# Two tiles of heads in one burst of the scan's products, in a one-core decoder trunk

## The chip, the core and the metric

The kernel runs on one core of a Trainium2 chip. The metric is the time of one execution on the device in microseconds (us), the median of several runs. TensorE does the matmuls (PE in the rows; PEld is its weight load), VectorE (DVE), ScalarE (ACT) and GpSimd (POOL) the elementwise work, and the queue of SyncE (SP) issues the DMAs.

## What is computed

Two layers over 512 tokens of width 2048. The first has a Mamba-2 mixer, the second stick-breaking attention; after each mixer comes a gated embedding. The change is in the first layer's mixer, which has 8 groups of 8 heads of 64 channels and works in 4 chunks of 128 tokens. Cut to what matters of the reference:

```
scores = einsum("bclgn,bcsgn->bclsg", cm, bm)
y_diag = einsum("bclsg,bclsgr,bcsgrp->bclgrp", scores, decay, xdt)
chunk_states = einsum("bclgn,bclgr,bclgrp->bcgrpn", bm, decay_to_end, xdt)
prev_states = scan(state * chunk_decay + chunk_states)
y_off = einsum("bclgn,bcgrpn,bclgr->bclgrp", cm, prev_states, exp(acum))
y = (y_diag + y_off + d_skip * xs) * silu(z)
y = y * rsqrt(mean(y * y over the group) + eps) * gnorm_w;  out = y @ out_w
```

`decay` is exp of the difference of two cumulative sums where the row is not before the column, else 0.

## The kernel before

All activations lie with channels on the partitions and the 512 tokens along the free dimension. A projection is split into units: one unit makes 128 output channels, and has 16 blocks of 128 input channels, each with three matmuls of 512 columns (high and low parts of weight and activation in fp32r, `mm3`). Weights come in halves of 8 blocks (512 KB, `block`): a DMA into `raw` (two buffers), a cast by ScalarE to `wh`, a difference by VectorE to `wl` (three buffers each). These matmuls write tiles named mm.

The order on TensorE is written out by hand by the class `Flow`. It queues every matmul behind the one before, counts a planned time for each (512/2370 = 0.216 for an mm or for a product in fp32 of 128 columns; one product in fp32 shows as two MATMULs in the trace), and after every three mm asks its jobs (`poll`). A job is a generator: it yields a planned delay and is resumed at the first poll after it. The delay counts from before the resumed piece of work. The order of the other engines' instructions, and of the DMAs on SP's queue, is set by the framework's scheduler.

For each group of heads the loop does units for B, C and four tiles of x (`conv`), then spawns the job `scan`, and goes on with four units for the gate z (`zs[0]` to `zs[3]`), the next group's units or, after the last group, the first half of the output projection `w_out`, whose activations `staged` loads back from DRAM (y_d), into the buffers of xc. So the scan's pieces of work lie between mm of other units.

The scan transposes x (px_x), makes the scores (px_sc), transposes B (px_bt) and makes the states (px_st, kept as `sts`). Then, for each of four tiles `i` of two heads each:

- for each of two heads: a DMA of one row of `ac_d`, broadcast to all partitions, into `ab` (two buffers); M by ScalarE from it (L411 four times, L414), times the masked scores scT by VectorE (L415); half of `eA` by ScalarE (L417, two buffers). M has four buffers, which the group norm's `sh` and `sl` share.
- a delay of 9.0, and a wait until `zs[i]` is there;
- a burst on TensorE: 8 products of y (px_y, 64 weight columns each, two heads side by side) and 3 of the states (px_o);
- eA times px_o (VectorE, L433), `y` from xc and px_y (VectorE, L436), their sum (GpSimd, L437), times zs (VectorE, L438), its square (ScalarE) and the sum of squares `sacc` (GpSimd).

After the four tiles come a delay of 8.5, one of 3.5, and the group norm (px_gn). All px tiles share four PSUM buffers of one bank each.

Of the kernel before, what the change touches and what calls it, by code (L numbers as in the profile page):

```python
# [9 lines left out]
F32 = mybir.dt.float32  # L10
F32R = mybir.dt.float32r
AF = mybir.ActivationFunctionType
ALU = mybir.AluOpType
# [3 lines left out]
P = 128  # L17
T = 512
# [3 lines left out]
HG = 8  # L22
NH = 64
NC = 4
# [58 lines left out]
def trunk(  # L83
    ctx: ExitStack, tc: tile.TileContext, xT, pT, vecs, hvecs, consts, w_dt, w_in, w_out, w_sb, w_v, w_sbo, w_gate, w_ple, out
):
    nc = tc.nc
    V, S, G = nc.vector, nc.scalar, nc.gpsimd
    fl = Flow(tc)
# [11 lines left out]
    ac_d = dram.tile([NH, T], F32, name="ac_d")  # L100
    h_d = dram.tile([EARLY * P, T], F32, name="h_d")

    def px(name="px"):
        return pxp.tile([P, T], F32, tag="px", name=name)
# [14 lines left out]
    dsk = vec[:, 96:128]  # L119
# [20 lines left out]
    def split(dst_h, dst_l, src, scale=None):  # L140
        if scale is None:
            S.copy(dst_h, src)  # L142
            V.tensor_tensor(dst_l, src, dst_h.bitcast(F32), op=ALU.subtract)  # L143
        else:
            S.activation(dst_h, src, AF.Copy, scale=scale)
            V.scalar_tensor_tensor(dst_l, src, scale, dst_h.bitcast(F32), op0=ALU.mult, op1=ALU.subtract)  # L146
# [73 lines left out]
    with ExitStack() as st:  # L220
        sp = st.enter_context(tc.tile_pool(name="sp", bufs=1))

        def tmp(name):
            return sp.tile([P, T], F32, tag="tmp", name=name, bufs=3)
# [4 lines left out]
        for k in range(KT):  # L229
# [16 lines left out]
            else:  # L246
                sq = tmp("sq")
# [22 lines left out]
        act_ = sp.tile([P, NC, NH], F32, name="act_")  # L270
# [71 lines left out]
        def scan(g, BT, CT, xc, zs):  # L342

            hs = slice(g * HG, (g + 1) * HG)
            yield 11.0
            xdt, xw = [], []
            for c in range(NC):
                pt = px("px_x")
                for i in range(4):
                    fl.transpose(pt[:, i * P : (i + 1) * P], xc[i][:, c * P : (c + 1) * P], ident)  # L350
                xd = sp.tile([P, HG, 64], F32, tag=f"xdt{c}", name=f"xdt{c}")
                V.tensor_tensor(
                    xd,
                    pt.rearrange("p (h q) -> p h q", q=64),
                    dtt[:, c, hs].unsqueeze(2).broadcast_to([P, HG, 64]),
                    op=ALU.mult,
                )
                xdt.append(xd)
                if c < NC - 1:
                    w_ = sp.tile([P, HG, 64], F32, tag="xw", name="xw")  # L360
                    G.tensor_tensor(w_, xd, dte[:, c, hs].unsqueeze(2).broadcast_to([P, HG, 64]), op=ALU.mult)
                    wh_ = sp.tile([P, T], F32R, tag="xwh", name="xwh")
                    wl_ = sp.tile([P, T], F32R, tag="xwl", name="xwl")
                    split(wh_, wl_, w_.rearrange("p h q -> p (h q)"))
                    xw.append((wh_, wl_))
                if c == 1:

                    pss = px("px_sc")
                    for c_ in range(NC):
                        cs = slice(c_ * P, (c_ + 1) * P)  # L370
                        fl.mm(pss[:, cs], BT[:, cs], CT[:, cs])
                    scT = sp.tile([P, NC, P], F32, tag="scT", name="scT")
                    V.tensor_tensor(
                        scT, pss.rearrange("p (c l) -> p c l", l=P), tri.unsqueeze(1).broadcast_to([P, NC, P]), op=ALU.mult
                    )
                    psb = px("px_bt")
                    for c_ in range(NC - 1):
                        fl.transpose(psb[:, c_ * P : (c_ + 1) * P], BT[:, c_ * P : (c_ + 1) * P], ident)
                    Bh = sp.tile([P, (NC - 1) * P], F32R, tag="Bh", name="Bh")
                    Bl = sp.tile([P, (NC - 1) * P], F32R, tag="Bl", name="Bl")  # L380
                    split(Bh, Bl, psb[:, : (NC - 1) * P])
                yield 4.0
                if c >= 1:

                    e = c - 1
                    pst = px("px_st")
                    es = slice(e * P, (e + 1) * P)
                    mm3(pst, Bh[:, es], Bl[:, es], xw[e][0], xw[e][1])
                    sc = sp.tile([P, HG, 64], F32, tag=f"st{e}", name=f"st{e}")
                    if e == 0:  # L390
                        sts = [sc]
                        V.tensor_copy(sc, pst.rearrange("p (h q) -> p h q", q=64))
                    else:
                        G.tensor_tensor(sc, sts[-1], cdb[:, e, hs].unsqueeze(2).broadcast_to([P, HG, 64]), op=ALU.mult)
                        V.tensor_tensor(sc, pst.rearrange("p (h q) -> p h q", q=64), sc, op=ALU.add)
                        sts.append(sc)
                    yield 1.0

            sacc = sp.tile([P, T], F32, tag="sacc", name="sacc")
            ys = []  # L400
            for i in range(4):
                eA = sp.tile([P, T - P], F32, tag="eA", name="eA", bufs=2)
                Ms = []
                for hh in range(2):
                    h = g * HG + 2 * i + hh
                    ab = sp.tile([P, T], F32, tag="ab", name="ab", bufs=2)
                    nc.sync.dma_start(ab, ac_d[h : h + 1, :].broadcast_to([P, T]))
                    M = sp.tile([P, NC, P], F32, tag="Mt", name="M", bufs=4)

                    for c in range(NC):  # L410
                        S.activation(  # L411
                            M[:, c, :], ab[:, c * P : (c + 1) * P], AF.Relu, bias=act_[:, c, h : h + 1], scale=-1.0
                        )
                    S.activation(M, M, AF.Exp, scale=-1.0)  # L414
                    V.tensor_tensor(M, M, scT, op=ALU.mult)  # L415
                    pp = slice(64 * hh, 64 * hh + 64)
                    S.activation(eA[pp, :], ab[pp, P:], AF.Exp)  # L417
                    Ms.append(M)
                yield 9.0
                while zs[i] is None:  # L420
                    yield 1.0
                psy = px("px_y")
                for c in range(NC):
                    for hh in range(2):
                        fl.mm(psy[64 * hh : 64 * hh + 64, c * P : (c + 1) * P], xdt[c][:, 2 * i + hh, :], Ms[hh][:, c, :])
                pso = px("px_o")
                for c in range(1, NC):
                    fl.mm(
                        pso[:, (c - 1) * P : c * P],
                        sts[c - 1].rearrange("p h q -> p (h q)")[:, i * P : (i + 1) * P],  # L430
                        CT[:, c * P : (c + 1) * P],
                    )
                V.tensor_tensor(eA, pso[:, : T - P], eA, op=ALU.mult)  # L433
                y = sp.tile([P, T], F32, tag="y", name="y", bufs=2)
                u = 4 * g + i
                V.scalar_tensor_tensor(y, xc[i], dsk[:, u : u + 1], psy, op0=ALU.mult, op1=ALU.add)  # L436
                G.tensor_tensor(y[:, P:], y[:, P:], eA, op=ALU.add)  # L437
                V.tensor_tensor(zs[i], y, zs[i], op=ALU.mult)  # L438
                ys.append(zs[i])
                if i == 0:  # L440
                    S.activation(sacc, ys[i], AF.Square)
                else:
                    sq = tmp("sq")
                    S.activation(sq, ys[i], AF.Square)
                    G.tensor_tensor(sacc, sacc, sq, op=ALU.add)
            yield 8.5
            psn = px("px_gn")
            sh = sp.tile([P, T], F32R, tag="Mt", name="sh", bufs=4)
            sl = sp.tile([P, T], F32R, tag="Mt", name="sl", bufs=4)
            split(sh, sl, sacc)  # L450
            yield 3.5
            mm2(psn, r512, sh, sl)
            rg = sp.tile([P, T], F32, tag="rg", name="rg")
            rsqrt(rg, psn, eps6[:, 1:2])
            for i in range(4):
                u = 4 * g + i
                V.scalar_tensor_tensor(ys[i], ys[i], gnw[:, u : u + 1], rg, op0=ALU.mult, op1=ALU.mult)
                nc.sync.dma_start(y_d[u * P : (u + 1) * P, :], ys[i])

        for g in range(NG):  # L460
            u0, c0 = 10 * g, 6 * g
            BT = sp.tile([P, T], F32, tag="BT", name="BT", bufs=2)
            CT = sp.tile([P, T], F32, tag="CT", name="CT", bufs=2)
# [4 lines left out]
            xc = []  # L468
# [5 lines left out]
            zs = [None] * 4  # L474
# [20 lines left out]
    h = []  # L495
# [316 lines left out]
```

## Time and profile before

| | us |
|---|---|
| median of 3 runs | 2749.87 |
| lowest and highest | 2748.03, 2751.34 |
| profiled execution | 2750.45 |
| its span, first to last instruction | 2748.6 |
| TensorE busy in it | 2729.6 (99%) |
| VectorE, ScalarE, GpSimd busy | 1519.1, 1262.0, 362.1 |

A row of the timeline has start, duration, engine, line, operation, output and inputs, the number of equal instructions in a row, and in brackets the engine's idle time before it with what ended it. Matmuls overlap: the distance of two starts is what TensorE pays, not the duration. Grouped rows have busy time, mean ns of one, and idle time before them.

### The profile page before, as it was taken

The page shows a single profiled execution, that of the slowest core. Times are in us where ns is not written, and L with a number is a line of the kernel's source. Part 1 is how long each engine was busy: PE and PEld are TensorE (multiplying, and loading weights), DVE is VectorE, ACT ScalarE, POOL GpSimd, SP SyncE. Part 2 cuts the span into 40 slices and gives each one's busy share as a digit, 9 for nine tenths or more (in the row PEclk, how much of TensorE's full clock was granted, in tenths as well). Part 3 has the DMA queues.
Part 4 walks back from the last instruction along what each step waited for, and adds up shares of the span by engine and source line. Part 5 has one row for each costly group of instructions (what it writes and reads, how often), then busy time and mean ns, then how long its engine had stood idle before and what let it go on. Part 6 is the DMA issues. An engine that isn't in the chain of part 4 may idle for free.

```text
span 2748.6 us, 32580 instructions
## 1 busy us (share of the span) xinstructions
PE 2729.6 (99%) x12684; PEld 2248.5 (82%) x12684; DVE 1519.1 (55%) x1970; ACT 1262.0 (46%) x1956; POOL 362.1 (13%) x363
## 2 busy tenths in 40 slices
PE   8999999999999999999999999999999999999999
PEld 6888888888888878888888888888888888888887
DVE  8565665665565673342433547647647657643533
ACT  6464545546464552232433436646546546533321
POOL 2222221212222120001100100000000000011000
PEclk9999999999999999999999999999999999999999
DMA  4342333333242446343233322322232322332332
GB/s 160 109 131 93 130 100 123 100 113 124 96 131 98 142 141 222 94 145 93 92 100 100 94 98 90 95 89 91 82 96 85 92 91 86 113 124 97 107 117 90
DMA packets 98346, 300.52 MB, mean 109 GB/s; under 512 B 10960, under 2 KB 11088, under 8 KB 98192
## 3 DMA queue, kind: packets, MB, share of 16 engines
q1 hardware_dynamic: 98192, 298.44, 33.7%
q8 instruction: 99, 1.62, 0.2%
q14 instruction: 55, 0.45, 0.1%
HBM read 280.18 MB, written 18.22 MB: 109 GB/s over the span
## 4 chain that ended last, share of the span: by engine, by line
PE 96%; DMA 1%; DVE 1%; ACT 1%; issue 0%; POOL 0%; SPq 0%; DVEq 0%
PE mm L54 80%; PE pv L54 6%; PE px_p L54 2%; PE px_r L54 1%; PE px_y L54 1%; PE px_z L54 1%; PE px_av L54 1%; PE px_o L54 1%; DMA stg<-y_d 1%; PE px_st L54 1%; PE px_qn L54 1%; PE px_x L57 1%; PE psB L54 0%; PE psd L54 0%; DVE al L146 0%; DVE al L143 0%
## 5 line engine op out<-in xcount | busy, mean ns | idle before, releaser
L54 PE MATMUL mm<-ah,wh 128*128 128x512 f32 x3312 | 1301.0, 393 | 1.7 <-ACT ah L142 1.7
L54 PE MATMUL mm<-ah,wl 128*128 128x512 f32 x3312 | 1292.2, 390 | 0.0
L54 PE MATMUL mm<-al,wh 128*128 128x512 f32 x3312 | 1290.4, 390 | 0.8 <-DVE al L143 0.8
L135 ACT CAST wh<-raw 128x1024 fp32r<-128x1024 f32 x457 | 479.1, 1049 | 840.8 <-PE mm L54 714.2
L137 DVE TENSOR_TENSOR wl<-raw,wh 128x1024 fp32r<-128x1024 f32 x457 | 568.8, 1245 | 530.2 <-ACT wh L135 529.4
L54 PEld LDWEIGHTS mm<-ah,wl 128*128 128x128 f32 x3312 | 621.9, 188 | 132.0
L54 PEld LDWEIGHTS mm<-al,wh 128*128 128x128 f32 x3312 | 622.5, 188 | 129.4 <-DVE al L143 2.1
L54 PEld LDWEIGHTS mm<-ah,wh 128*128 128x128 f32 x3312 | 622.4, 188 | 128.5 <-ACT ah L142 2.8
L503 POOL TENSOR_TENSOR ssq<-ssq,sq 128x512 f32<-128x512 f32 x45 | 71.6, 1590 | 619.9 <-ACT sq L502 619.9
L339 DVE SCALAR_TENSOR_TENSOR cv<-xr,vec,cv 128x512 f32<-128x512 f32 x144 | 108.7, 755 | 2.9
L650 POOL TENSOR_SCALAR_AFFINE_SELECT lm<-lm 128x128 f32<-128x128 f32 x64 | 28.1, 439 | 615.6 <-DVE lm L649 609.8
L54 PE MATMUL pv<-wh,ah 128*128 128x512 f32 x256 | 101.0, 395 | 0.4 <-DVE gt L532 0.4
L54 PE MATMUL pv<-wl,ah 128*128 128x512 f32 x256 | 99.9, 390 | 0.0
L54 PE MATMUL pv<-wh,al 128*128 128x512 f32 x256 | 99.7, 389 | 0.0
L411 ACT ACTIVATE M<-ab,act__370 128x128 f32<-128x128 f32 x256 | 83.7, 389 | 32.5 <-PE px_y L54 31.2
L203 ACT ACTIVATE sg<-cv 128x512 f32<-128x512 f32 x48 | 30.3, 632 | 122.0 <-DVE cv L339 121.8
L532 DVE TENSOR_TENSOR gt<-mm,rbc 128x512 f32<-128x512 f32 x32 | 22.1, 691 | 103.9 <-PE mm L54 103.9
L205 POOL TENSOR_TENSOR xc<-cv,sg 128x512 f32<-128x512 f32 x32 | 42.7, 1334 | 263.8 <-ACT sg L204 263.8
L647 DVE SCALAR_TENSOR_TENSOR lb<-px_z,e 128x128 f32<-128x128 f32 (+1 forms) x64 | 31.4, 490 | 72.7 <-ACT e L645 72.1
L415 DVE TENSOR_TENSOR M<-M,scT 128x512 f32<-128x512 f32 x64 | 58.5, 923 | 14.0 <-ACT M L414 13.8
L205 POOL TENSOR_TENSOR zs<-zs,sg 128x512 f32<-128x512 f32 x32 | 44.7, 1396 | 139.6 <-ACT sg L204 128.7
L335 DVE TENSOR_TENSOR xr<-mm,rbc 128x512 f32<-128x512 f32 x47 | 32.4, 689 | 52.7 <-PE mm L54 52.7
(219 smaller groups left out, 2546.1 us busy)
## 6 DMA issues: line engine op xcount, KB each, us to landing
raw<-in_w_in SPq DMA_DIRECT2D x160, 512.0 KB, 3.6
raw<-in_w_sb SPq DMA_DIRECT2D x96, 512.0 KB, 3.5
raw<-in_w_out SPq DMA_DIRECT2D x64, 512.0 KB, 3.9
raw<-in_w_gate SPq DMA_DIRECT2D x64, 512.0 KB, 3.5
ab<-ac_d SPq DMA_DIRECT2D x64, 256.0 KB, 3.3
raw<-in_w_v SPq DMA_DIRECT2D x32, 512.0 KB, 3.5
raw<-in_w_sbo SPq DMA_DIRECT2D x32, 512.0 KB, 3.5
y_d<-zs SPq DMA_DIRECT2D x32, 256.0 KB, 3.8
```

What stands on the lines that cost most here:

```text
L54: self._queue(self.tc.nc.tensor.matmul(out, lhsT, rhs, start=start, stop=stop), rows / 2370.0)
L135: S.copy(wh, raw)
L137: V.tensor_tensor(wl, raw, wh.bitcast(F32), op=ALU.subtract)
L203: S.activation(tmp, half, AF.Tanh)
L205: G.tensor_tensor(dst, half, tmp, op=ALU.mult)
L335: V.tensor_tensor(xr[:, 3 : T + 3], ps, rbc, op=ALU.mult)
L339: V.scalar_tensor_tensor(cv, xr[:, tap : tap + T], cw[:, u, tap : tap + 1], cv, op0=ALU.mult, op1=ALU.add)
L411: S.activation(M[:, c, :], ab[:, c * P : (c + 1) * P], AF.Relu, bias=act_[:, c, h : h + 1], scale=-1.0)
L415: V.tensor_tensor(M, M, scT, op=ALU.mult)
L503: G.tensor_tensor(ssq, ssq, sq, op=ALU.add)
L647: V.scalar_tensor_tensor(lb, pz, 0.0, e, op0=ALU.min, op1=ALU.subtract)
L650: G.affine_select(out=lm[:, :P], in_=lm[:, :P], compare_op=ALU.is_gt, fill=0.0, base=0, pattern=[[1, P]], channel_multiplier=-1,)
```

## The change

The loop over four tiles becomes a loop over two pairs. M of all four heads of a pair is made first; the delay is 16.0 before the first pair and 18.0 before the second, and the wait is for the second tile's zs. Then one burst has the 8 products of y of the one tile, those of the other, and the 3 products of the states of the one and of the other, in four PSUM tiles. The elementwise work follows for each of the two tiles, with the same instructions. The numbers of buffers stay.

```diff
-            for i in range(4):
-                eA = sp.tile([P, T - P], F32, tag="eA", name="eA", bufs=2)
-                Ms = []
-                for hh in range(2):
...
-                    Ms.append(M)
-                yield 9.0
-                while zs[i] is None:
-                    yield 1.0
-                psy = px("px_y")
-                for c in range(NC):
-                    for hh in range(2):
-                        fl.mm(psy[64 * hh : 64 * hh + 64, c * P : (c + 1) * P], xdt[c][:, 2 * i + hh, :], Ms[hh][:, c, :])
-                pso = px("px_o")
-                for c in range(1, NC):
-                    fl.mm(
-                        pso[:, (c - 1) * P : c * P],
...
-                V.tensor_tensor(eA, pso[:, : T - P], eA, op=ALU.mult)
...
+            for i0 in (0, 2):
+                eAs, Ms = [], []
+                for i in (i0, i0 + 1):
+                    eA = sp.tile([P, T - P], F32, tag="eA", name="eA", bufs=2)
+                    for hh in range(2):
+                        h = g * HG + 2 * i + hh
+                        ab = sp.tile([P, T], F32, tag="ab", name="ab", bufs=2)
+                        nc.sync.dma_start(ab, ac_d[h : h + 1, :].broadcast_to([P, T]))
+                        M = sp.tile([P, NC, P], F32, tag="Mt", name="M", bufs=4)
...
+                        Ms.append(M)
+                    eAs.append(eA)
+                yield 18.0 if i0 else 16.0
+                while zs[i0 + 1] is None:
+                    yield 1.0
+                psys = [px("px_y") for _ in range(2)]
+                for q in range(2):
+                    for c in range(NC):
+                        for hh in range(2):
+                            fl.mm(
+                                psys[q][64 * hh : 64 * hh + 64, c * P : (c + 1) * P],
+                                xdt[c][:, 2 * (i0 + q) + hh, :],
+                                Ms[2 * q + hh][:, c, :],
+                            )
+                psos = [px("px_o") for _ in range(2)]
+                for q in range(2):
+                    for c in range(1, NC):
+                        fl.mm(
+                            psos[q][:, (c - 1) * P : c * P],
...
+                for q in range(2):
+                    i = i0 + q
+                    eA = eAs[q]
+                    V.tensor_tensor(eA, psos[q][:, : T - P], eA, op=ALU.mult)
...
+                    G.tensor_tensor(y[:, P:], y[:, P:], eA, op=ALU.add)
+                    V.tensor_tensor(zs[i], y, zs[i], op=ALU.mult)
...
```

## Rows read from the trace of the kernel before

**Rows 1.** The page: the chain that ended last, by engine.
```profile
PE 96%; DMA 1%; DVE 1%; ACT 1%; issue 0%; POOL 0%; SPq 0%; DVEq 0%
```

**Rows 2.** Timeline of TensorE around the first burst of the fourth group.
```profile
504.58 0.39 PE L54 MATMUL mm<-ah,wl 128*128 128x512 f32 x1
504.90 1.09 PE L54 MATMUL px_y<-M,xdt 128*64 128x128 f32 x16
505.93 0.94 PE L54 MATMUL px_o<-CT,st 128*128 128x128 f32 x6
...
506.93 0.39 PE L54 MATMUL mm<-al,wh 128*128 128x512 f32 x1
...
509.24 0.39 PE L54 MATMUL mm<-ah,wl 128*128 128x512 f32 x1
```

**Rows 3.** Timeline, 444 to 453: first and last of 40 mm.
```profile
444.03 0.39 PE L54 MATMUL mm<-ah,wl 128*128 128x512 f32 x1
...
452.87 0.39 PE L54 MATMUL mm<-ah,wl 128*128 128x512 f32 x1
```

**Rows 4.** Groups by shape on TensorE, whole span: busy us, mean ns, idle us.
```profile
L54 PE MATMUL px_y<-M,xdt 128*64 128x128 f32 x512 | 35.0, 279 | 0.0
L54 PE MATMUL px_o<-CT,st 128*128 128x128 f32 x192 | 29.9, 292 | 0.0
...
L54 PE MATMUL px_sc<-CT,BT 128*128 128x128 f32 x64 | 8.5, 275 | 0.0
```

**Rows 5.** Timeline of TensorE where the scores pass into the transposes of B.
```profile
479.86 1.06 PE L54 MATMUL px_sc<-CT,BT 128*128 128x128 f32 x8
480.75 0.49 PE L57 MATMUL px_bt<-cst,BT 128*128 128x128 f32 x3
```

**Rows 6.** The page: casts of weights by ScalarE; loads of ab, us to landing.
```profile
L135 ACT CAST wh<-raw 128x1024 fp32r<-128x1024 f32 x457 | 479.1, 1049 | 840.8 <-PE mm L54 714.2
...
ab<-ac_d SPq DMA_DIRECT2D x64, 256.0 KB, 3.3
```

**Rows 7.** Timeline of TensorE in the last group's scan.
```profile
994.97 1.09 PE L54 MATMUL px_y<-M,xdt 128*64 128x128 f32 x16
...
1018.13 0.39 PE L54 MATMUL mm<-ah,wl 128*128 128x512 f32 x1
...
1019.78 0.50 PE L54 MATMUL mm<-al,wh 128*128 128x512 f32 x1 [0.33 <-DVE al L143]
```

**Rows 8.** Busy us (instructions) of PE, PEld, DVE, ACT, POOL in one stretch.
```profile
505.90:524.80 18.90, 18.90 (x113) 15.33 (x111) 11.78 (x14) 14.35 (x31) 5.29 (x4) 1.00 0.45 133
```

**Rows 9.** Timeline of ScalarE there: casts of staged tiles.
```profile
1011.00 2.19 ACT L142 CAST ah<-stg 128x512 fp32r<-128x512 f32 x4 [2.26 <-DMA stg<-y_d]
...
1018.27 1.27 ACT L142 CAST ah<-stg 128x512 fp32r<-128x512 f32 x2 [1.10 <-DMA stg<-y_d]
```

**Rows 10.** Instructions that touch M: ns min/median/max, first and last start.
```profile
L415 DVE TENSOR_TENSOR M<-M,scT x64: 675/693/1789, 114.5 to 1022.0; 128x512 f32<-128x512 f32 x64
```

**Rows 11.** Timeline of the vector engines from the same burst on.
```profile
506.03 1.57 ACT L411 ACTIVATE M<-ab,act__370 128x128 f32<-128x128 f32 x5 [1.72 <-PE px_y L54]
...
506.90 0.56 DVE L433 TENSOR_TENSOR eA<-px_o,eA 128x384 f32<-128x384 f32 x1
...
507.51 0.62 ACT L414 ACTIVATE M<-M 128x512 f32<-128x512 f32 x1
507.54 1.02 POOL L437 TENSOR_TENSOR y<-y,eA 128x384 f32<-128x384 f32 x1 [1.87 <-DVE eA L433]
...
508.59 0.53 ACT L417 ACTIVATE eA<-ab 64x384 f32<-64x384 f32 x1 [0.47 <-POOL y L437]
...
515.44 1.28 ACT L411 ACTIVATE M<-ab,act__370 128x128 f32<-128x128 f32 x4 [2.75 <-PE px_y L54]
...
519.46 1.54 POOL L445 TENSOR_TENSOR sacc<-sacc,sq 128x512 f32<-128x512 f32 x1 [1.47 <-ACT sq L444]
...
519.76 1.78 DVE L415 TENSOR_TENSOR M<-M,scT 128x512 f32<-128x512 f32 x1
```

More of the change, by code (lines that the diff above doesn't have):

```diff
@@ L400, in scan @@
             ys = []
-            for i in range(4):
-                eA = sp.tile([P, T - P], F32, tag="eA", name="eA", bufs=2)
-                Ms = []
-                for hh in range(2):
[L405 to L408, printed above, removed]
-                    for c in range(NC):
-                        S.activation(
-                            M[:, c, :], ab[:, c * P : (c + 1) * P], AF.Relu, bias=act_[:, c, h : h + 1], scale=-1.0
-                        )
[L414 to L417, printed above, removed]
-                    Ms.append(M)
-                yield 9.0
-                while zs[i] is None:
-                    yield 1.0
-                psy = px("px_y")
-                for c in range(NC):
-                    for hh in range(2):
-                        fl.mm(psy[64 * hh : 64 * hh + 64, c * P : (c + 1) * P], xdt[c][:, 2 * i + hh, :], Ms[hh][:, c, :])
-                pso = px("px_o")
-                for c in range(1, NC):
-                    fl.mm(
-                        pso[:, (c - 1) * P : c * P],
-                        sts[c - 1].rearrange("p h q -> p (h q)")[:, i * P : (i + 1) * P],
-                        CT[:, c * P : (c + 1) * P],
-                    )
-                V.tensor_tensor(eA, pso[:, : T - P], eA, op=ALU.mult)
[L434 to L445, printed above, removed]
@@ new lines, in scan @@
+            for i0 in (0, 2):
[8 more added lines that the diff above has]
+                        for c in range(NC):
+                            S.activation(
+                                M[:, c, :], ab[:, c * P : (c + 1) * P], AF.Relu, bias=act_[:, c, h : h + 1], scale=-1.0
+                            )
+                        S.activation(M, M, AF.Exp, scale=-1.0)
+                        V.tensor_tensor(M, M, scT, op=ALU.mult)
+                        pp = slice(64 * hh, 64 * hh + 64)
+                        S.activation(eA[pp, :], ab[pp, P:], AF.Exp)
+                        Ms.append(M)
[5 more added lines that the diff above has]
+                for q in range(2):
+                    for c in range(NC):
+                        for hh in range(2):
[3 more added lines that the diff above has]
+                                Ms[2 * q + hh][:, c, :],
+                            )
+                psos = [px("px_o") for _ in range(2)]
[3 more added lines that the diff above has]
+                            psos[q][:, (c - 1) * P : c * P],
+                            sts[c - 1].rearrange("p h q -> p (h q)")[:, (i0 + q) * P : (i0 + q + 1) * P],
+                            CT[:, c * P : (c + 1) * P],
+                        )
+                for q in range(2):
+                    i = i0 + q
+                    eA = eAs[q]
+                    V.tensor_tensor(eA, psos[q][:, : T - P], eA, op=ALU.mult)
+                    y = sp.tile([P, T], F32, tag="y", name="y", bufs=2)
+                    u = 4 * g + i
+                    V.scalar_tensor_tensor(y, xc[i], dsk[:, u : u + 1], psys[q], op0=ALU.mult, op1=ALU.add)
+                    G.tensor_tensor(y[:, P:], y[:, P:], eA, op=ALU.add)
+                    V.tensor_tensor(zs[i], y, zs[i], op=ALU.mult)
+                    ys.append(zs[i])
+                    if i == 0:
+                        S.activation(sacc, ys[i], AF.Square)
+                    else:
+                        sq = tmp("sq")
+                        S.activation(sq, ys[i], AF.Square)
+                        G.tensor_tensor(sacc, sacc, sq, op=ALU.add)
```

## Prediction

> **What bounds the kernel.** I read the chain that ended last first: 96% of it is TensorE, and the vector engines have 1% each [rows 1]. So time is won only where TensorE issues its work faster, or lost where it waits. The profiled run took 2750.45 us for a span of 2748.6, 0.02% above the median of 2749.87; I make the sum in differences and apply it to the median.
>
> The next view is the timeline of TensorE around one burst of the scan [rows 2]. A projection matmul (mm) starts every 0.2267 us where nothing is in its way (39 starts in 8.84 us, [rows 3]). In a burst a product in fp32 appears as two MATMULs: 8 products of y are 16 MATMULs with 64 weight columns, 3 products of the states are 6 MATMULs with 128. From the last mm start before it (504.58) to the second after it (506.93) are 2.35 us; two mm starts would take 0.453, so the burst costs 1.90 us. There are 32 of them (512 MATMULs of px_y, [rows 4]).
>
> **What a burst costs at its borders.** By the grouped lines [rows 4] the 16 MATMULs of px_y are busy 35.0/32 = 1.094 us per burst, so they start (1.094 - 0.273)/15 = 54.7 ns apart. The pace of 128x128 in fp32 I take from px_sc, which comes 8 in a row: (8.5/8 - 0.275)/7 = 112.5 ns. At these paces a burst would be 16 x 0.0547 + 6 x 0.1125 = 1.55 us. So 1.90 - 1.55 = 0.35 us go at its borders, mm to px_y, px_y to px_o, px_o to mm. Is it the change of tile or the change of shape that costs? Where px_sc passes into px_bt [rows 5], output, PSUM buffer and operands change and the shape stays: eight starts, the one over the border among them, take 0.89 us, 0.111 each. So a new tile of the same shape costs nothing there, and what costs in a burst I take to be the change from 128 weight columns to 64 and back.
>
> After a burst mm is slow for a while: the ten starts from 506.93 to 509.24 take 2.31 us in place of 2.27, 0.04 more [rows 2].
>
> **The change, part by part.** The sixteen merged bursts do the same 704 MATMULs. Each merge puts 22 MATMULs inside a burst that exists, at 1.55 us, in place of 1.90 + 0.04 for one of its own.
>
> Borders: 16 x 0.35 = 5.5 us less. From below the border between the two tiles of heads could cost as much as that between shapes (nothing saved); the nearest row [rows 5] has it at nothing, so I take 5.5.
>
> The slow mm after a burst: between 0 and 16 x 0.04 = 0.7 us less. If it grew with the number of MATMULs in the burst, a merge would save none of it. I take it as a price per burst, 0.7, since it is spent after the burst, on mm that are the same either way.
>
> The trace's pace inside a burst stands against the Trainium skill's "TensorE: Matmul & The Clock Gate", section "Back-to-back issue gap", which gives about 81 ns per matmul for a stream of weight loads and matmuls of 128 columns. By that figure 22 MATMULs more would be an estimated 1.78 us, a merge would save 0.16 us and the kernel 2.6; the trace has 54.7 and 112.5 ns for these shapes, and I go by it.
>
> Vector, ScalarE and GpSimd do the same instructions. The eight loads of ab in a group stay too, on SP's queue; the third and fourth of the second half now wait for the first burst. A load of weights queued behind such a wait comes later, and that is hidden: ScalarE's 457 casts of weights stand 714 us, 1.6 each, waiting for TensorE to give back a buffer [rows 6], and with three buffers a cast block is used some two blocks (24 mm, 5.4 us each) after; only a delay beyond that would reach TensorE. PSUM: a merged burst takes all four px buffers; the last product before it (px_st) lies 17 plan us earlier and the next (px_gn) 8.5 + 3.5 later, so none is waited for. Nothing is costed there.
>
> When the bursts come follows from the plan: an mm counts 512/2370 = 0.216 there, three make a step of 0.648. A 16.0 in place of 9.0 is 25 steps for 14, so the first burst of the group of [rows 2] moves from 504.90 by 11 steps, 33 mm, 7.5 us, to 512.4. A merged burst's 22 products count 22 x 0.216 = 4.75 in the plan; of 18.0 there remain 13.25, 21 steps, 63 mm, 14.3 us. With the burst's own 3.5 us the second comes 17.8 us after the first.
>
> The last group is the only place where TensorE already waits in this part: from 1018.13 two starts take 1.65 us in place of 0.45, for the staged tiles of y_d [rows 7], 1.2 us lost. Its first burst, now at 994.97 [rows 7], moves to about 1002.4, the second to 1020.2, and ScalarE must now do, from 1003.6 on (when px_y gives M's buffers back), the work that took it 14.35 busy us in an earlier group [rows 8] and the last seven casts of staged tiles (4, 1 and 2 in three rows, of which [rows 9] has the first and the last), 0.6 each, 4.1 in all. That ends at 1022.0, with the product with scT (0.69 at the median, [rows 10]) at 1022.7; the second half of the burst needs it at 1021.1. So it is 1.6 us late, of which 1.2 is the wait that is there already: 0.4 us more. The bounds: 1.2 less if the staged tiles come in time, 3.3 more if the last staged load slips behind one of ab (both are 256 KB, and ab takes 3.3 us to land, [rows 6]). I take 0.5.
>
> Sum: -5.5 - 0.7 + 0.5 = -5.7; 2749.9 - 5.7 = 2744.2 us.
>
> **Rival 1, slower: the second burst waits for M.** Four M are made between the bursts in place of two, because there are four buffers and all are held until px_y. The path after the first burst's start, by [rows 2, 6, 10, 11]: px_o starts 1.03 us after px_y, now 1.03 + 0.87 = 1.9; the first tile's px_o 0.94; eA on VectorE 0.56; y on GpSimd 1.02; eA on ScalarE 0.53, which frees an ab buffer; the load, 3.3 us to landing; two M at 5 starts in 1.57 us and an exp of 0.62, some 1.8 each, and an eA between, 4.1; a cast of weights 1.0; the product with scT 0.69. With the gaps between them 14.3 us, against 17.8 + 0.9 (the second tile's px_y is half a burst later): over 4 us to spare. By ScalarE's load it is tighter: from 1.13 us after the burst's start to 18.7 are 17.5 us, for 14.35 us of work and 0.69: 2.5 to spare. Against it: in 505.9 to 524.8 that work took 18.9 us with its idle time [rows 8], which would be 2.1 us too late; but 2.75 of that idle time were the wait for the second burst's px_y [rows 11], which is gone. Each us too late costs 8 us, one per group; at 0.7 us the whole gain is gone, at 1.4 it is slower by over 0.2%. At 2.1 us the time is 2744.2 + 17 = 2761. One thing can add to it: the product with scT takes 1.79 us at most [rows 10], and the one of 1.78 at 519.76 ran beside an addition of GpSimd [rows 11]; with two tiles' additions at once the last one may take 1.1 us longer, which leaves 1.4 to spare.
>
> The Trainium skill's "SBUF — State Buffer", section "Who interferes with whom", says that a VectorE instruction with two SBUF inputs contends with a GpSimd instruction that reads SBUF, and that the second blocks until the first is done; the pair of 519.76 agrees. I give this rival 0.16.
>
> **Rival 2: the merge doesn't save the border.** If the 0.35 us belong to each tile (its operands, its PSUM bank) and not to the change of shape, they stand again inside the merged burst; only 0.7 - 0.5 remain, 2749.7. The rows of the border inside one shape [rows 5] speak against it, but no row shows 32 MATMULs with 64 columns in a row. 0.08.
>
> **Rival 3: the last group eats it.** The last staged load comes 3.3 us later: 2749.9 - 6.2 + 3.3 = 2747.0. For it: TensorE waits for these tiles as it is [rows 7], and SP's queue has ab loads among theirs. Against it: ScalarE, free of M until 1003.6, can cast staged tiles before. 0.16.
>
> **The numbers.** 0.60 for the forecast, with its own range 2742.5 (the 1.2 us gone too) to 2746. I put the line between faster and same at 0.2%, 5.5 us, about what a measurement of this kernel tells from no change: 2744.4. Three quarters of the forecast's 0.60 lie below it: 0.45 faster. Same: 0.15 of the forecast, rivals 2 and 3 and a small part of rival 1: 0.41. Slower: 0.14. The range leaves out the worse half of rival 1 and less than 1 in 10 below: 2742.0 to 2752.0.
>
> **What would show it.** Merged bursts of 32 and 12 MATMULs that cost 3.45 us from the last mm to the second after, less two mm; px_y starts 54.7 ns apart throughout; 63 mm between the bursts of a group. It would be wrong if TensorE shows idle time before px_y that ends with VectorE's M (rival 1), if a gap stands at the middle of the 32 (rival 2), or if TensorE's wait for ah and al near 1018 grows (rival 3).

## The result and the profile after

The changed kernel takes 2777.08 us (median of 5 runs, 2773.85 to 2779.55), the kernel before 2749.87: a ratio of 1.0101, 95% interval 1.009 to 1.0112. The forecast was 2744.2 us. The profiled execution took 2773.85 us for a span of 2771.8, 23.2 us more than before, with a mean granted clock of 0.996. It is the shortest of the five: the median is 27.2 us above the kernel before, and the longer executions, with mean granted clocks of 0.994 to 0.996, have no trace. What follows accounts for the 23.2.

The chain that ended last is no longer nearly all TensorE; 7% of it now lies on VectorE and ScalarE (96% TensorE in [rows 1]):

```profile
PE 91%; DVE 4%; ACT 3%; DMA 1%; issue 1%; POOL 0%; SPq 0%; POOLq 0%; DVEq 0%
```

The timeline of TensorE around the first burst of the fourth group answers to [rows 2]:

```profile
518.66 0.39 PE L54 MATMUL mm<-ah,wl 128*128 128x512 f32 x1
518.98 1.97 PE L54 MATMUL px_y<-M,xdt 128*64 128x128 f32 x32
520.87 1.60 PE L54 MATMUL px_o<-CT,st 128*128 128x128 f32 x12
522.23 0.48 PE L54 MATMUL mm<-ah,wh 128*128 128x512 f32 x1
522.55 0.39 PE L54 MATMUL mm<-al,wh 128*128 128x512 f32 x1
```

From the last mm before the burst to the second after it are 3.89 us, less two mm 3.44; the forecast was 3.45. The second burst starts at 536.72, 17.7 us later (forecast 17.8), and no burst of the kernel waits for M. So the burst did what it was to do. The loss stands in the waits of TensorE (us in total, times, longest):

```profile
PE px_gn L54 <- ACT sh L142: 9.2, 7, 1.4
...
PE mm L54 <- ACT ah L142: 5.0, 2, 4.5
PE px_gn L54 <- DVE sl L143: 3.8, 7, 0.5
PE mm L54 <- DVE al L143: 2.6, 4, 1.6
```

The waits for sh and sl are new. They are those of the group norm's product. The timeline of the fourth group before (TensorE, the making of sh and sl):

```profile
534.16 0.94 PE L54 MATMUL px_o<-CT,st 128*128 128x128 f32 x6
...
536.83 1.01 POOL L437 TENSOR_TENSOR y<-y,eA 128x384 f32<-128x384 f32 x1
...
540.89 0.62 ACT L142 CAST sh<-sacc 128x512 fp32r<-128x512 f32 x1 [1.65 <-POOL sacc L445]
...
541.54 0.69 DVE L143 TENSOR_TENSOR sl<-sacc,sh 128x512 fp32r<-128x512 f32 x1 [1.84 <-ACT sh L142]
...
545.87 0.39 PE L54 MATMUL px_gn<-sh,cstr 128*128 128x512 f32 x1
```

and after, with the clock's fall behind it:

```profile
538.62 1.60 PE L54 MATMUL px_o<-CT,st 128*128 128x128 f32 x12
...
543.03 1.98 POOL L448 TENSOR_TENSOR y<-y,eA 128x384 f32<-128x384 f32 x2
...
546.37 2.64 POOL L456 TENSOR_TENSOR sacc<-sacc,sq 128x512 f32<-128x512 f32 x2 [1.36 <-ACT sq L455]
...
548.03 0.39 PE L54 MATMUL mm<-ah,wl 128*128 128x512 f32 x1
549.71 0.50 PE L54 MATMUL px_gn<-sh,cstr 128*128 128x512 f32 x1 [1.29 <-ACT sh L142]
550.74 0.50 PE L54 MATMUL px_gn<-sl,cstr 128*128 128x512 f32 x1 [0.54 <-DVE sl L143]
551.08 0.39 PE L54 MATMUL mm<-ah,wh 128*128 128x512 f32 x1
...
551.78 0.62 PE L54 MATMUL mm<-ah,wh 128*128 128x512 f32 x1
552.20 0.63 PE L54 MATMUL mm<-al,wh 128*128 128x512 f32 x1
```

Before, sl was done at 542.2, 3.6 us ahead of the product's place at 545.87. After, the product's place comes 36 mm behind the burst in place of 48, 2.7 us sooner, since the delay of 8.5 counts from before the burst and a merged burst uses up 4.75 of it in place of 2.4. And its operands come 3.3 us later, counted from the end of the last px_o: the work of two tiles stands one behind the other, where one tile's stood. The sum of y and eA on GpSimd ends 4.8 us behind px_o in place of 2.7, which is 2.1 of the 3.3, and the rest comes up to sacc, sh and sl. 3.6 - 2.7 - 3.3 = 2.4 us too late. In starts: 1.68 + 1.03 us in place of 0.235 + 0.229, 2.25 us lost, in seven groups, 15.8 us. In four of them mm then starts every 0.427 us for a while, at a granted clock of 0.50 (1.2 GHz), which costs 8 x 0.2 = 1.6 us each. The window view shows it (span; busy and instructions of PE, PEld, DVE, ACT, POOL; granted clock): from the second group's px_sc to the third's, from the third's to the fourth's, and the stretch behind the fourth's wait:

```profile
236.72:360.80 124.08, 122.24 (x609) 100.77 (x608) 74.85 (x89) 63.52 (x108) 28.43 (x22) 1.00 0.34 111
360.80:486.46 125.66, 123.84 (x609) 101.91 (x608) 74.52 (x89) 63.39 (x108) 28.39 (x22) 0.99 0.34 109
551.80:555.10 3.30, 3.30 (x9) 2.65 (x8) 0.94 (x1) 3.25 (x6) 0.00 (x0) 0.50 0.69 256
```

The first of these stretches has a wait and no fall of the clock, the second has both and is 1.6 us longer, and in the third the clock is at half. From px_sc to px_sc the seven groups take 124.1 us three times and 125.7 to 125.8 four times.

The last group has no wait at the norm, but long ones for the staged tiles. TensorE and ScalarE there:

```profile
1032.68 0.40 PE L54 MATMUL mm<-ah,wl 128*128 128x512 f32 x1
...
1034.08 1.26 ACT L412 ACTIVATE M<-ab,act__370 128x128 f32<-128x128 f32 x4
...
1036.96 2.16 ACT L142 CAST ah<-stg 128x512 fp32r<-128x512 f32 x4
...
1037.62 0.80 PE L54 MATMUL mm<-ah,wh 128*128 128x512 f32 x1 [4.54 <-ACT ah L142]
```

and SP's queue before that:

```profile
1018.45 4.91 SPq L160 DMA_DIRECT2D stg<-y_d  x6
1026.94 0.32 SPq L408 DMA_DIRECT2D ab<-ac_d  x1
...
1028.01 0.32 SPq L408 DMA_DIRECT2D ab<-ac_d  x1
```

ScalarE casts the next staged tiles (1036.96, with no wait for a DMA in the row) only behind the M of the second pair, whose loads of ab are issued at 1026.9 and 1028.0, and two starts of TensorE lie 4.9 us apart. In all its starts lose 8.0 us there in place of 1.2 [rows 7], and from 1037 to 1043 the clock is at 0.50, which costs some 1.7 us more.

The sum in spans: -6.2 for the borders (16 x 0.39), +15.8 for the norm's waits, +6.4 for the four stretches at half clock, +6.8 + 1.7 for the last group. That is +24.5. A wait with such a stretch in the attention layer, at 2367 us of the trace before (TensorE idle for 1.28 and 0.23 us), is shorter after (0.47 and 0.22) and has no fall of the clock: -2.4. So 22.1 of the 23.2 us are named. That wait lies outside the change and differs from run to run, as experiment 8 shows.

### The profile page after: what moved, and what is told of

Same layout as the page of the kernel before. It is cut to its first block, busy times and chain, and to the rows that moved or that the text cites. A ratio compares the mean times of both kernels' runs of the same rounds, so it can differ in the third digit from the quotient of the medians.

```text
span 2771.8 us, 32608 instructions
## 1 busy us (share of the span) xinstructions
PE 2734.3 (99%) x12684; PEld 2254.6 (81%) x12684; DVE 1526.0 (55%) x1970; ACT 1261.2 (46%) x1956; POOL 370.6 (13%) x363
## 4 chain that ended last, share of the span: by engine, by line
PE 91%; DVE 4%; ACT 3%; DMA 1%; issue 1%; POOL 0%; SPq 0%; POOLq 0%; DVEq 0%
PE mm L54 76%; PE pv L54 6%; PE px_p L54 2%; PE px_r L54 1%; DVE wl L137 1%; PE px_z L54 1%; PE px_av L54 1%; ACT wh L135 1%; ACT M L412 1%; PE px_st L54 1%; PE px_y L54 1%; DVE cv L339 1%; PE px_qn L54 1%; PE px_x L57 1%; DMA stg<-y_d 0%
## 5 line engine op out<-in xcount | busy, mean ns | idle before, releaser
L137 DVE TENSOR_TENSOR wl<-raw,wh 128x1024 fp32r<-128x1024 f32 x457 | 577.0, 1263 | 569.4 <-ACT wh L135 563.4
L543 DVE TENSOR_TENSOR gt<-mm,rbc 128x512 f32<-128x512 f32 x32 | 22.1, 691 | 103.9 <-PE mm L54 103.9
L416 DVE TENSOR_TENSOR M<-M,scT 128x512 f32<-128x512 f32 x64 | 50.2, 795 | 14.1 <-ACT M L415 13.7
L54 PEld LDWEIGHTS pv<-wh,ah 128*128 128x128 f32 x256 | 48.1, 188 | 10.3 <-DVE gt L543 0.8
```

The costliest lines, as they stand in the source:

```text
L54: self._queue(self.tc.nc.tensor.matmul(out, lhsT, rhs, start=start, stop=stop), rows / 2370.0)
L137: V.tensor_tensor(wl, raw, wh.bitcast(F32), op=ALU.subtract)
```

## The experiments

All ratios are to the kernel before, timed beside each run (2748.72 to 2749.18 us).

**1. The norm's product later.** One number of the changed kernel:

```diff
-            yield 8.5
+            yield 13.0
             psn = px("px_gn")
```

> Theory (the group norm's product px_gn is queued on TensorE before its operands sh and sl are there, because its delay counts from before the merged burst): with 13.0 in place of 8.5 the product comes seven steps of three mm later, the waits of 7 x 2.3 us = 16 us go, and with them the stretches at half clock that follow four of them, 4 x 1.6 us; the time is 2777 - 22 = 2755 us, and what is left over the kernel before is the last group. Rival (pairs load ScalarE and VectorE so much that the work behind a burst is late wherever the product stands): the wait moves along with the product and the time stays above 2770 us.

2751.28 us, ratio 1.0008 (1.0 to 1.0017): 25.8 us less than the changed kernel, for 22 expected; the 22 were worked out from the profiled execution, which is 3.2 us below the median. The profile has no wait for sh or sl, and a group takes 121.71 us from px_sc to px_sc, at a clock of 1.00, where the kernel before takes 122.52:

```profile
112.73:234.44 121.71, 121.71 (x608) 100.84 (x607) 74.13 (x89) 63.28 (x108) 28.15 (x22) 1.00 0.34 113
```

```profile
112.30:234.82 122.52, 122.52 (x609) 100.65 (x608) 73.85 (x89) 63.73 (x108) 27.35 (x22) 1.00 0.35 112
```

So two merges save 0.81 us, 0.40 each; the forecast was 0.35 + 0.04. The rival of a loss that moves along with the product is out. The last group still waits for its staged tiles, up to 4.5 us at a time, and this eats the gain of all the others.

**2. The last group in single bursts too.** Pairs in seven groups, with 13.0; in the last the four bursts of before:

```diff
+            n2 = 1 if g == NG - 1 else 2
+            for i0 in range(0, 4, n2):
...
+                yield 9.0 if n2 == 1 else 18.0 if i0 else 16.0
...
+            yield 8.5 if n2 == 1 else 13.0
```

> The same delay of 13.0, and the last group as in the kernel before: four bursts of one tile, delays 9.0 and 8.5. Theory (what is left after the norm is the last group, where the making of M stands ahead of the casts of staged tiles in ScalarE's order): only the borders of fourteen merged bursts remain, 14 x 0.39 = 5.4 us less than the kernel before, 2744.5 us. Rival (a loss in every group that the waits of TensorE do not show): above 2749.9 us.

2743.27 us, ratio 0.9981 (0.9972 to 0.9989): 5.6 us less than the kernel before beside it, for 5.4 expected. In its trace each of the seven groups takes 121.70 us from px_sc to px_sc, 0.82 less than before, 5.7 in all. So with the two late waits gone, merging gives what its borders cost. The two profiled spans differ in other places too, but none that the edit touches: 1.7 us more before the first group, 2.8 less at the wait in the attention layer.

**3. The kernel before, with the norm's product early.** No merging; the same line from 8.5 to 2.7:

> The kernel before, with single bursts, and one number changed: 2.7 in place of 8.5 ahead of the norm, nine steps earlier, 6.1 us, where it has 3.6 us to spare now. Theory: a wait of about 2.4 us in each group, 8 x 2.4 = 19 us, and stretches at half clock behind some of them, 1.6 us each: 2769 to 2782 us, without a merged burst. Rival (the loss needs the merged bursts, or the clock falls because of them): no more than 2769 us and a clock as before.

2777.55 us, ratio 1.0104 (1.009 to 1.0118), as slow as the change itself. That the two times agree is chance: here are eight waits and seven stretches at half clock, and neither the borders' gain nor the last group's loss. The waits of TensorE, and one of them with what follows:

```profile
PE px_gn L54 <- ACT sh L142: 12.8, 8, 1.6
...
PE px_gn L54 <- DVE sl L143: 2.1, 8, 0.5
```

```profile
300.83 0.50 PE L54 MATMUL px_gn<-sh,cstr 128*128 128x512 f32 x1 [1.63 <-ACT sh L142]
301.56 0.50 PE L54 MATMUL px_gn<-sl,cstr 128*128 128x512 f32 x1 [0.23 <-DVE sl L143]
...
302.67 0.63 PE L54 MATMUL mm<-ah,wh 128*128 128x512 f32 x1
303.09 0.63 PE L54 MATMUL mm<-al,wh 128*128 128x512 f32 x1
```

The starts lose 2.28 us in each of the first seven groups, and behind all seven the clock is at 0.50 for a while (mm every 0.43 us). So neither the wait nor the fall of the clock needs a merged burst; a late product of two matmuls is enough.

**4. The order inside the merged burst.** The kernel of run 2, with the products of the second tile behind the states of the first:

```diff
+                for q in range(n2):
+                    psys.append(px("px_y"))
+                    psos.append(px("px_o"))
+                    for c in range(NC):
+                        for hh in range(2):
+                            fl.mm(
+                                psys[q][64 * hh : 64 * hh + 64, c * P : (c + 1) * P],
...
+                    for c in range(1, NC):
+                        fl.mm(
+                            psos[q][:, (c - 1) * P : c * P],
...
```

> The kernel of the run above with the last group single, but in a merged burst the order is y and states of the one tile, then y and states of the other. If a change of the weights' shape is what costs at a border, each of the fourteen bursts has two borders more, 14 x 0.35 = 4.9 us over that kernel, and the gain is all but gone: 2749.4 us. If merging alone saves (fewer changes between mm and the burst), some of it stays, the time lies between 2744.5 and 2749.4 us. The profile shows the price of the border from px_o to px_y by itself.

2747.61 us, ratio 0.9995 (0.9986 to 1.0004), 4.3 us over run 2. The timeline of one burst, and one group in the window view:

```profile
511.61 0.39 PE L54 MATMUL mm<-ah,wl 128*128 128x512 f32 x1
511.93 1.09 PE L54 MATMUL px_y<-M,xdt 128*64 128x128 f32 x16
512.96 0.94 PE L54 MATMUL px_o<-CT,st 128*128 128x128 f32 x6
513.82 1.09 PE L54 MATMUL px_y<-M,xdt 128*64 128x128 f32 x16
514.84 0.94 PE L54 MATMUL px_o<-CT,st 128*128 128x128 f32 x6
515.53 0.48 PE L54 MATMUL mm<-ah,wh 128*128 128x512 f32 x1
515.85 0.40 PE L54 MATMUL mm<-al,wh 128*128 128x512 f32 x1
```

```profile
112.32:234.69 122.37, 122.37 (x608) 100.97 (x607) 74.19 (x89) 63.53 (x108) 27.23 (x22) 1.00 0.33 112
```

The burst takes 4.24 us from the last mm to the second after, 0.35 more than with the states at the end, and the group 122.37 us, within 0.15 of the kernel before. The same MATMULs in a merged burst save next to nothing when the shape changes four times; what costs is the change between 64 and 128 weight columns, not the border to mm as such nor the tile. Start by start, a change to 64 columns costs 0.14 us, from mm and from px_o alike, one from 64 to 128 costs 0.20, and the border from px_o to mm, 128 to 128, nothing (under 0.01). The Trainium skill's "TensorEngine Tiling (Array Packing)", section "Key Properties", says that a change of the tiling mode, and not of the tile, drains TensorE; this run agrees as far as the price goes, with 0.17 us for each such change added within a burst (0.35 / 2), and doesn't show whether it is a drain.

**5. The staged tiles' casts first.** The kernel of run 1, with the loads and splits of the staged tiles at a higher priority:

```diff
-        acts = staged(sp, [(f"xc{i}", 2) for i in range(4)], y_d, 0, KT)
+        with tc.high_priority(offset=4000):
+            acts = staged(sp, [(f"xc{i}", 2) for i in range(4)], y_d, 0, KT)
```

> The first run's kernel (norm later, pairs in all groups) with the loading back and splitting of the staged tiles at a higher priority, so that in the last group ScalarE casts them ahead of the making of M. Theory (in ScalarE's fixed order the casts of the last staged tiles stand behind M of the second pair, for which the loads of ab come late): TensorE's waits for staged tiles, 8 us in that run, and the 6.8 us at half clock behind them (3.4 us lost) go; 2751.3 - 8 - 3 = 2741 us if the second burst still finds its M, up to 2746 if it waits for them. Rival (the staged loads themselves come late behind ab on SP's queue): the order of the casts changes nothing, 2750 to 2752 us.

2744.68 us, ratio 0.9986 (0.9978 to 0.9995), 6.6 us less than run 1. The waits for the staged tiles are gone, the clock doesn't fall there, and one other wait has come in the last group (the second row is the attention layer's wait, at 2365):

```profile
PE px_y L54 <- DVE M L416: 2.2, 1, 2.2
PE mm L54 <- ACT ah L142: 0.9, 1, 0.9
```

This is rival 1 of the prediction in the last group: the burst stands after 18 of its 32 MATMULs and waits for the second tile's M. So ScalarE's order was what the staged tiles waited for. The edit moves their loads forward too, but before it the late casts had no wait for a DMA. With a merged burst one of the two, staged tiles or M, was late in either order.

**6. The last group's bursts earlier.** The kernel of run 1, with 9.0 in place of 16.0 ahead of the first burst of the last group:

```diff
-                yield 18.0 if i0 else 16.0
+                yield 18.0 if i0 else 9.0 if g == NG - 1 else 16.0
```

> The first run's kernel with 9.0 in place of 16.0 ahead of the first merged burst of the last group alone, so that both its bursts and the making of M come 7.5 us earlier, when the projection out has not begun. Theory: M of the second pair is made before the staged tiles are wanted, the waits go for the most part, 2742 to 2745 us. Rival (the waits come from SP's queue): they stay, 2750 to 2752 us. A risk: the first burst finds fewer of its M ready and waits for them itself.

2751.38 us, ratio 1.0007 (0.9998 to 1.0016): no better than run 1, and my expectation was wrong. The runs lie in two groups, five from 2748.1 to 2749.5 and six from 2751.4 to 2752.2; the profiled one, 2749.4, is of the first, and what the others lose more isn't shown. SP's queue now issues the staged loads one by one behind those of ab and of weights:

```profile
991.04 3.97 SPq L160 DMA_DIRECT2D stg<-y_d  x5
997.14 0.32 SPq L408 DMA_DIRECT2D ab<-ac_d  x1
998.37 0.32 SPq L160 DMA_DIRECT2D stg<-y_d  x1
...
1001.71 0.33 SPq L133 DMA_DIRECT2D raw<-in_w_out  x1
1003.41 0.32 SPq L160 DMA_DIRECT2D stg<-y_d  x1
```

In the last group TensorE's waits for ah and al come to 4.7 us, where run 1's profile has 6.7, and one stretch at half clock is left. How much of it is this queue and how much the order of ScalarE is open.

**7. A shorter wait at the norm.** The changed kernel with 9.8 in place of 8.5:

> The changed kernel with 9.8 in place of 8.5 ahead of the norm, two steps (1.4 us) later: a wait of about 1.1 us in each of seven groups in place of 2.4. If the clock falls only where the wait is long, there is no stretch at half clock in those groups: 2777 - 7 x 1.4 - 6.4 = 2761 us. If every wait there lets it fall, the half clock stays at 1.6 us in four or more groups: 2767 us or more.

2759.58 us, ratio 1.004 (1.0026 to 1.0054). The starts lose 0.9 to 1.4 us in each of seven groups, and in none of them the clock falls: the first group takes 122.69 us at 1.00.

```profile
112.61:235.30 122.69, 122.16 (x608) 100.78 (x607) 74.81 (x89) 63.75 (x108) 28.11 (x22) 1.00 0.34 112
```

So at this place the half clock came with the longer wait alone, and a wait of 2.3 us costs up to 3.9.

**8. Runs 2 and 5 together.**

> The second run's kernel (norm later, last group single) with the staged tiles at the higher priority of the fifth run. The wait for staged tiles that is left in the second run (1.0 us in the last group) should go; 2743.3 - 1.0 = 2742.3 us. If the single bursts then wait for M in its place, as the merged burst of the fifth run did for 2.2 us, no gain or a loss of 1 to 2 us.

2743.35 us, ratio 0.9978 (0.9969 to 0.9987), not to be told from run 2, for 2742.3 expected. The first row is run 2's wait in the last group, the second a wait in this run's attention layer:

```profile
1015.58 0.50 PE L54 MATMUL mm<-al,wh 128*128 128x512 f32 x1 [0.85 <-DVE al L143]
```

```profile
2363.39 0.49 PE L54 MATMUL mm<-ah,wh 128*128 128x512 f32 x1 [0.92 <-ACT ah L142]
```

The wait in the last group is gone: TensorE waits there neither for staged tiles nor for M. But in the attention layer it waits 0.92 us for ah, where run 2's profile has no such wait. That wait stands outside the edits and varies between the profiles: 1.28 us in the kernel before, 0.47 in the changed one, 0.2 in run 1, 0.9 in run 5, 0.5 in run 6. Its cause is open, and so is whether it is what hid the gain in the median.

## Why the prediction was wrong

**The borders** were right: 3.44 us a merged burst for 3.45, 0.40 us a merge in run 1, 5.6 us in run 2. Rival 2 is out by the burst of 32 without a gap and by run 4. The slow mm after a burst don't grow with it, as taken: over ten starts they cost 0.025 us after a merged burst (median of 16), 0.041 after a single one. The 54.7 ns from px_y to px_y are a mean: the starts come in twos, 7 and 102 ns apart, before and after alike, which changes no sum.

**The step that failed** stands in "The change, part by part", where PSUM is asked about: "the next (px_gn) 8.5 + 3.5 later, so none is waited for. Nothing is costed there." I asked of px_gn only whether its PSUM buffer would be free, not whether its operands would be there. Both halves of the answer were at hand. I had worked out that a merged burst uses up 4.75 of the delay behind it, and applied it to the 18.0 ahead of the second burst, but not to the 8.5 behind it. And two tiles' chains of VectorE, GpSimd and ScalarE now end together; I priced the first tile's chain up to eA, for the M that follow, and not the second's up to sacc. With 3.6 us of slack before, both together make it 2.4 late. Run 1 shows the cause by taking it away, run 3 by making it without the change. It costs 15.8 us, and 6.4 more through the clock, which the prediction had no term for.

**The last group** was mis-sized: +0.5 us taken, with 3.3 as the upper bound, and 8.5 measured (6.8 + 1.7). The price of rival 3 was a late load of 3.3 us; run 5 shows that the casts' place in ScalarE's order was the cause: in the changed kernel they stand behind M whose loads of ab come at 1026.9 and 1028.0. My count of ScalarE's work gave an end 1.6 us late, but a sum of busy time says nothing on which of two things waits in a fixed order. Moved earlier (run 6) the median is no better.

**Rival 1** didn't come in the eight groups: the last M was ready about 0.9 us ahead of the second burst of the fourth group (the last product with scT starts at 535.13 and takes 0.69; px_y starts at 536.72) and 1.9 us ahead of the 19th MATMUL, where run 5's burst waited for it; that is tighter than the 2.5 I gave. It came in run 5 where other work was put first.

## What to carry to other kernels

When work on the bounding engine is gathered into a longer piece, look at what stands behind that piece in a hand-made order: a delay that counts planned time shrinks by the piece's own length, and the work that follows from it comes in one batch, so its last result is later. Read the slack of the next product (its place less the end of its operands) in the trace before, and take both shifts from it. A change of the weights' shape on TensorE has a price each way, so group products by shape; here 0.17 us a change on average.

## What the runs showed of the hardware

A wait that cost TensorE 2.24 to 2.37 us in starts, with one short matmul in the middle, was followed by a stretch at half clock (granted clock 0.50) in 4 of 7 places (the change) and in 7 of 8 (run 3); one of 0.9 to 1.4 us in none of 7 (run 7). Its length alone doesn't decide: 2.4 us inside a burst in run 5, and 2.4 us at 1021 in run 6, were followed by none, and the two waits in the attention layer of the kernel before, 1.28 and 0.23 us idle, by one (mm every 0.427 us from 2370.9). What decides is open. A stretch made a group 1.6 us longer. I had taken an idle time as costing its own length.
